# The vector c on ScalarE's queue, x's first block ahead of the first weights, gate rows through DRAM, and less VectorE work in softmax and rope, in a two-layer hybrid attention trunk

## The chip, the cores and the metric

The kernel runs on one core of one Trainium2 chip. The metric is the device time of one execution in microseconds. TensorE (PE; its weight loads are PEld), VectorE (DVE), ScalarE (ACT), GpSimd (POOL) and SyncE (SP) each run their own list of instructions in order and wait for one another by semaphores; DMAs are issued from a queue of SyncE or ScalarE.

## What is computed

Two layers over x (256 tokens of width 1024), each with its own weights. This is the reference, cut to what the change and the steps of the prediction touch:

```python
def hybrid_layer(x, c, w_ada, b_ada, w_in, ...):
    shift, scale, gate = jnp.split(c @ w_ada + b_ada, 3, axis=-1)
    u = x * (1.0 + scale[:, None, :]) + shift[:, None, :]
    h = split_cols(u @ w_in)          # 4,080 columns: three attention groups and a gate path
    ...                               # rope on most queries and keys; 4 + 6 + 6 heads
    y = (mix * jax.nn.silu(h["gate"])) @ w_out
    return layer_norm(ALPHA * x + (1.0 + gate[:, None, :]) * y, ln_g, ln_b)

def masked_softmax(s, mask):
    s = jnp.where(mask, s.astype(jnp.float32), -jnp.inf)
    m = jnp.max(s, -1, keepdims=True)
    m = jnp.where(jnp.isfinite(m), m, 0.0)
    e = jnp.where(mask, jnp.exp(s - m), 0.0)
    return e / jnp.maximum(jnp.sum(e, -1, keepdims=True), 1e-30)

def rope(x, pos):
    ...
    x1, x2 = x[..., :half], x[..., half:]
    return jnp.concatenate([x1 * cos - x2 * sin, x1 * sin + x2 * cos], -1).astype(x.dtype)
```

The three groups are DSA (4 heads, a learned index picks 64 of the keys), FoX (6 heads with a decay from a running sum) and NSA (6 heads, three branches: compressed, selected and window). All is float32.

## The kernel before

**Weights.** All weights lie in one DRAM stream `wst`, in pieces of up to 1024 columns over 128 partitions (512 KB). `stream_order` (L180) fixes their order, `load_more` (L475) issues them on SyncE's queue into 11 raw slots, a piece each time that a slot is freed. Small inputs stand in `fixed` and go on the same queue, where the order has them: x transposed in four blocks of 256 KB (`xt`, j = 0, 2, 4, 6), each behind the first projection piece of its j; tables and masks after them.

**Products.** A product in float32 is made of three passes in the rounded type: the raw piece is cast to a high half `wh` on ScalarE (`split_hi`, L519), VectorE subtracts to get the low half `wl` (`split_lo`, L534), and `mm3` (L548) multiplies high by high (L549), high by low and low by high (L550, L551). At most 8 pieces are split ahead.

**Modulation.** c comes first of all DMAs (L423), four matmuls spread it over the partitions (`spread_c`, L554), ten matmuls on zeros follow as warm-up (L575). c @ w_ada is done on VectorE: one multiplication with accumulated sum for each piece (`ada_gemv`, L583), 48 in all: the 16 of layer 0's scale and shift interleave with the first projection in order of j, the 16 of layer 1 run in `ada_second`, the 8 gate ones of each layer in `gate_task` (L613). That last one adds the bias (L618), then builds the gate row, the same 1024 values on all partitions: 16 matmuls of a broadcast column with the identity (L625) into PSUM and two copies on ScalarE (L628). The row is read by `resid` (L1251), which multiplies the output projection by it. `u_first` makes uH and the residue uL of u in layer 0 (L1370, L1372), `next_u` and `u_block` those of layer 1.

**Attention.** `attn_pair` treats two heads: scores, exponential with a running sum (`head_exp`, L680 to L697), `stats_finish` (L665: maximum with 1e-30, L667; reciprocal, L668; for NSA times its gate, L670), normalising on ScalarE (L710), transposes (L720, L724) and the product with the values (L773). There are 11 pairs in each layer; the compressed branch calls `stats_finish` too (`cmp_scores`). `rope` (L633) makes the product with the cosines (L641), two half-width products with the sines (L642, L643) and a sum (L644), 8 times in each layer.

**Order.** The instructions of all engines are written out by a planner, the class `Order`: every task is a generator that asks for an engine and a time; the planner keeps a clock for each engine from costs such as `rmm`, `cact` and `cvec`, and at each step lets the task of the best priority that can start go on (a smaller number comes first). What the tasks emit in that order is each engine's program. Priorities and the places of the loads are the entries of `PR` (L365). `split` is the priority of the two halves of a piece, as long as `nahead` pieces or more are ready ahead of TensorE (else it is -1); `gate` and `gate1` are those of `gate_task` in layers 0 and 1, `res` that of `resid`; `ada_at` says after which tile of layer 0 layer 1's modulation pieces are loaded; `tord` orders the 16 column tiles, `oq` the four quarters of the output projection.

Of the kernel before, what the change touches and what calls it, by code (L numbers as in the profile page):

```python
# [178 lines left out]

def stream_order():  # L180
# [14 lines left out]
    for l in range(DEPTH):  # L195
        if l == 0:
            ada(0, 0)
            for j in range(8):
                o.append((FIRST[j][0], 0, j))
                if j % 2 == 0:  # L200
                    o.append(("xt", j))
                o.extend((cc, 0, j) for cc in FIRST[j][1:])
                if j < 7:
                    ada(0, j + 1)
            o.append(("rope",))
        else:
            for c in PR["cord"]:
                chunk(c, l)
# [134 lines left out]
def rmm(cols, n=1):  # L343
    return n * cols / 2400.0
# [20 lines left out]
PR = dict(tout=(1, 1), tch=2, vmask=('', 'dnf'), zn='VV', upart=4, ul='VVVV', nrm='AAAA', cord='DCAB', t1q=0, cuts=(0, 512, 1024), oq=(0, 1, 2, 3), tord=(0, 1, 2, 3, 4, 5, 6, 7, 8, 9, 10, 11, 12, 13, 14, 15), gpp=(0, 1), res=-3.5, warm=10, tol=0.1, ada_at=[10, 0.5], adag_at=[[0, 0.5], [8, 1]], ow=(512, 256), aff=0.49, tw=512, nact=((0, 0), (1, 0), (0, 1), (1, 1)), pro='', gp0=(0, 1), gp1=(0, 1), acc=5, s=2, pt=1, o=3, ms=3, side=8, topk=3, idx=2, dec=0.5, cmp=1.2, nsa=1.6, dsa=1.7, fox=1.8, gate=4, gate1=6, ada=6, main=10, ev=0, split=4, nahead=2, acc1=1.5, cmp1=3, dec0=0.28, nsa1=5.08, topk1=5.9, nsa0=1.3, dec1=0.5, idx1=0.64, tord1=[2, 4, 6, 7, 0, 1, 8, 9, 5, 3, 14, 12, 10, 13, 11, 15], dsa0=1.48, oq0=(1, 0, 2, 3), cmp0=1.12, fox1=1.95, dsa1=4.17, fox0=1.48, oq1=[1, 3, 2, 0], topk0=3, tord0=[0, 1, 3, 4, 6, 7, 8, 9, 10, 11, 12, 13, 2, 5, 14, 15], idx0=2, nrm1='AAAA', nrm0='AAAA', t1q0=0, t1q1=0)  # L365
# [3 lines left out]
def trunk(ctx: ExitStack, tc: tile.TileContext, xT, x, crow, wst, bcol, lnrow, pe_b, cst, cstb, out,  # L369
# [9 lines left out]
    pp = ctx.enter_context(tc.tile_pool(name="pp", bufs=1, space=PSUM))  # L379
    ctx.enter_context(tc.manual_schedule())  # L380
# [42 lines left out]
    nc.sync.dma_start(c_row[0:P:32, 0:256], crow.rearrange("o (a b) -> (o a) b", b=256))  # L423
# [21 lines left out]
    for j in range(0, 8, 2):  # L445
        fixed["xt", j] = (xT_sb[:, j:j + 2, :], xT[:, j:j + 2, :])
# [28 lines left out]
    def load_more():  # L475
        while nload[0] < len(order):
            key = order[nload[0]]
            if key in fixed:
                nc.sync.dma_start(*fixed[key])
                dma[0] += 0.7  # L480
# [132 lines left out]
    def gate_task(l):  # L613
# [4 lines left out]
        V.tensor_tensor(m, m, bcol_sb[:, l, :, 2], op=ALU.add)  # L618
        Gr[l] = small([P, D], "row", 1, pool=act)
        for n in range(2):  # L620
            yield bank("ad")
            yield ("P", 4 * fmm(128))
            rows = ps(4, P)
            for i in range(4):
                T.matmul(rows[:, i, :], mods[l][:, 4 * n + i, 2:3].to_broadcast([P, P]), ident_f, start=True,  # L625
                         stop=True)
            yield ("A", cact(512))
            A.copy(Gr[l][:, 512 * n:512 * n + 512], rows.rearrange("p a b -> p (a b)"))  # L628
            unbank("ad")
            od.set("grow", l, n)  # L630


    def rope(dst, src, nh, dim, t, E=None):  # L633
# [8 lines left out]
        E.tensor_tensor(t3[:, :, :hf], x3[:, :, hf:], bcast(sinf[:, t, :hf], 1, nh), op=ALU.mult)  # L642
        E.tensor_tensor(t3[:, :, hf:], x3[:, :, :hf], bcast(sinf[:, t, hf:], 1, nh), op=ALU.mult)  # L643
# [59 lines left out]
    def head_pt(l, p_sb, r, a, ev, out_):  # L703
# [13 lines left out]
        yield ("P", 0.33)  # L717
# [11 lines left out]
    def attn_pair(l, kind, qT, kT, vs, obox, first, last, mask=None, cum=None, gate=None, prio=1):  # L729
# [30 lines left out]
        yield ("V", 0.35 + (0.12 if gate is not None else 0))  # L760
# [6 lines left out]
        yield ("P", fmm(128, 256))  # L767
# [19 lines left out]
    def layer(l, uH, uL):  # L787
# [111 lines left out]
        def idx_acc(acc, rl, hps, t, nk, before, ev):  # L899
# [595 lines left out]
```

## Time and profile before

| what | us |
|---|---|
| median of 3 runs | 360.07 (359.87 to 360.12) |
| the profiled execution | 359.52 |
| its span, first to last instruction | 357.7 |
| TensorE busy in it | 336.6 |
| VectorE busy | 312.4 |
| ScalarE busy | 249.8 |

The granted TensorE clock is 0.988 of full speed over the span. A matmul's recorded end is modelled and reaches into the next one, so TensorE's busy time shows where it stands still, and how dense its work is has to be read from the starts. Idle time of an engine counts only where the end hangs on it.

### The profile page before, as it was taken

The page shows a single profiled execution, that of the slowest core. Times are in us where ns is not written, and L with a number is a line of the kernel's source. Part 1 is how long each engine was busy: PE and PEld are TensorE (multiplying, and loading weights), DVE is VectorE, ACT ScalarE, POOL GpSimd, SP SyncE. Part 2 cuts the span into 40 slices and gives each one's busy share as a digit, 9 for nine tenths or more (in the row PEclk, how much of TensorE's full clock was granted, in tenths as well). Part 3 has the DMA queues.
Part 4 walks back from the last instruction along what each step waited for, and adds up shares of the span by engine and source line. Part 5 has one row for each costly group of instructions (what it writes and reads, how often), then busy time and mean ns, then how long its engine had stood idle before and what let it go on. Part 6 is the DMA issues. An engine that isn't in the chain of part 4 may idle for free.

```text
span 357.7 us, 6693 instructions
## 1 busy us (share of the span) xinstructions
PE 336.6 (94%) x2338; PEld 274.8 (77%) x2338; DVE 312.4 (87%) x811; ACT 249.8 (70%) x656; POOL 2.5 (1%) x10
## 2 busy tenths in 40 slices
PE   5899999999999999998998999999999999999990
PEld 1678789888887778695787878679798988788890
DVE  4798988999999989999999898998998989766485
ACT  3545565997868878998295875665998969998120
POOL 2000000000000000000000000000000000000000
PEclk9899999999999999999999999999999999999996
DMA  6999999996444667650588485552378724403011
GB/s 210 414 407 407 406 402 409 410 412 207 174 126 132 214 197 268 186 176 2 180 292 274 146 315 178 176 175 76 105 237 295 235 60 124 174 1 119 0 59 59
DMA packets 22073, 75.45 MB, mean 211 GB/s; under 512 B 2964, under 2 KB 3096, under 8 KB 21912
## 3 DMA queue, kind: packets, MB, share of 16 engines
q1 hardware_dynamic: 21752, 74.75, 59.5%
q8 instruction: 18, 0.29, 0.3%
q10 hardware_dynamic: 288, 0.29, 0.2%
q14 instruction: 15, 0.12, 0.1%
HBM read 73.98 MB, written 1.05 MB: 210 GB/s over the span
## 4 chain that ended last, share of the span: by engine, by line
PE 41%; DVE 7%; ACT 3%; issue 2%; DVEq 0%; ACTq 0%
PE b L549 10%; PE b L551 10%; PE b L550 10%; DVE wl L534 3%; PE b L773 2%; PE b L720 2%; PE b L739 2%; ACT p L686 1%; PE b L1030 1%; PE b L655 1%; PE b L926 1%; ACT p L710 1%; PE b L625 1%; DVE bn L1256 0%; DVE x_sb L1254 0%
## 5 line engine op out<-in xcount | busy, mean ns | idle before, releaser
L519 ACT CAST wh<-raw 128x1024 fp32r<-128x1024 f32 (+2 forms) x81 | 82.8, 1031 | 40.8 <-DMA raw<-in_wst_dram 25.0
L534 DVE TENSOR_TENSOR wl<-raw,wh 128x1024 fp32r<-128x1024 f32 (+2 forms) x81 | 96.2, 1194 | 10.2 <-ACT wh L519 4.9
L549 PE MATMUL b<-uH,wh 128*128 128x256 f32 x256 | 76.5, 299 | 0.0
L551 PE MATMUL b<-uH,wl 128*128 128x256 f32 x256 | 72.5, 283 | 0.0
L550 PE MATMUL b<-uL,wh 128*128 128x256 f32 x256 | 72.2, 282 | 0.0
L583 DVE SCALAR_TENSOR_TENSOR raw<-raw,cbc 128x1024 f32<-128x1024 f32 x48 | 58.1, 1217 | 3.2 <-DMA raw<-in_wst_dram 2.8
L549 PE MATMUL b<-wh,uH 128*128 128x512 f32 (+1 forms) x128 | 51.1, 400 | 2.3 <-ACT uH L1370 2.3
L551 PE MATMUL b<-wh,uL 128*128 128x512 f32 (+1 forms) x128 | 50.3, 393 | 2.4 <-DVE uL L1372 1.3
L549 PEld LDWEIGHTS b<-uH,wh 128*128 128x128 f32 x256 | 48.7, 190 | 3.4 <-issue 2.3
L550 PE MATMUL b<-wl,uH 128*128 128x512 f32 (+1 forms) x128 | 49.9, 389 | 0.0
L551 PEld LDWEIGHTS b<-uH,wl 128*128 128x128 f32 x256 | 48.7, 190 | 0.4 <-DVE wl L534 0.2
L550 PEld LDWEIGHTS b<-uL,wh 128*128 128x128 f32 x256 | 48.8, 191 | 0.0
L710 ACT ACTIVATE p<-p,rinv 128x128 f32<-128x128 f32 (+1 forms) x88 | 34.1, 449 | 5.6 <-DVE rinv L670 4.9
L551 PEld LDWEIGHTS b<-wh,uL 128*128 128x128 f32 x128 | 24.4, 191 | 9.0 <-DVE uL L1372 3.0
L549 PEld LDWEIGHTS b<-wh,uH 128*128 128x128 f32 x128 | 24.3, 190 | 7.5 <-ACT uH L1370 2.8
L550 PE MATMUL b<-wl,mH 128*128 128x512 f32 (+1 forms) x80 | 28.1, 351 | 1.6 <-DVE wl L534 1.6
L549 PE MATMUL b<-wh,mH 128*128 128x512 f32 (+1 forms) x80 | 28.5, 356 | 0.1
L551 PE MATMUL b<-wh,mL 128*128 128x512 f32 (+1 forms) x80 | 27.9, 349 | 0.3 <-DVE mL L1161 0.3
L550 PEld LDWEIGHTS b<-wl,uH 128*128 128x128 f32 x128 | 24.4, 191 | 4.1
L724 ACT COPY pT<-b 128x384 f32<-128x384 f32 x44 | 20.7, 478 | 4.7 <-PE b L720 4.3
L773 PE MATMUL b<-pT,vall 128*64 128x256 f32 (+1 forms) x176 | 21.7, 339 | 1.4 <-ACT pT L724 1.3
L720 PE MATMUL b<-cf,p 128*128 128x128 f32 x132 | 22.4, 281 | 0.5 <-ACT p L710 0.4
(178 smaller groups left out, 554.5 us busy)
## 6 DMA issues: line engine op xcount, KB each, us to landing
raw<-in_wst_dram SPq DMA_DIRECT2D x120, 512.0 KB, 4.9
raw<-in_wst_dram SPq DMA_DIRECT2D x7, 480.0 KB, 9.8
lnr<-in_lnrow_dram SPq DMA_DIRECT2D x4, 512.0 KB, 6.2
raw<-in_wst_dram SPq DMA_DIRECT2D x4, 448.0 KB, 4.4
xT_sb<-in_xT_dram SPq DMA_DIRECT2D x4, 256.0 KB, 9.5
x_sb<-in_x_dram SPq DMA_DIRECT2D x1, 1024.0 KB, 11.4
out_dram<-x_sb SPq DMA_DIRECT2D x3, 256.0 KB, 2.2
cf<-in_cst_dram SPq DMA_DIRECT2D x1, 384.0 KB
```

Source lines behind the costliest of these rows:

```text
L519: A.copy(h[:, :n], loaded[key])
L534: (G if on_pool else V).tensor_tensor(lo[:, :n], raw, h[:, :n].bitcast(F32), op=ALU.subtract)
L549: T.matmul(o, ah, bh, start=start, stop=False)
L550: T.matmul(o, ah, bl, start=False, stop=False)
L551: T.matmul(o, al, bh, start=False, stop=stop)
L583: V.scalar_tensor_tensor(w, w, 1.0, cbc, op0=ALU.mult, op1=ALU.mult, accum_out=mods[l][:, j, h:h + 1])
L625: T.matmul(rows[:, i, :], mods[l][:, 4 * n + i, 2:3].to_broadcast([P, P]), ident_f, start=True, stop=True)
L710: A.mul(blk, blk, r[:, t, a:a + 1])
L720: T.transpose(pt[:, i, :], p_sb[:, P * i:P * i + P], ident)
L724: A.copy(pT, pt.rearrange("p a b -> p (a b)"))
L739: T.matmul(sp[a][:, P * t:P * t + nk], qT[r, t * P:(t + 1) * P], kT[r, :nk], start=True, stop=onv and cum is None, skip_group_check=True)
L773: T.matmul(O[64 * a:64 * a + 64, P * kt:], vs(a, kt), outs[a][0][:, 256 * kt:256 + 128 * kt], start=(first and kt == 0), stop=(last and kt ...
```

## The change

- c's DMA is issued on ScalarE's queue, ahead of bcol's, and no longer on SyncE's.
- x transposed comes in five blocks, of 1, 2, 2, 2 and 1 of its eight parts (j = 0; 1 and 2; 3 and 4; 5 and 6; 7); the first, 128 KB, is issued ahead of the first projection weights, the others behind those of their first j.
- The gate row: after the bias is added, the 1024 values (8 in each partition, 3 apart) are written to a DRAM tile on SyncE's queue; about 4.5 us later by the planner's clock the tile is read back on the same queue, broadcast to all partitions (512 KB). The matmuls of L625 and the copies of L628 are gone.
- stats_finish takes the maximum with 1e-30 only for the compressed branch, where a row can be empty.
- rope makes one product of full width with the sines, over the two halves in reverse order, in place of two.
- The planner: TensorE's cost of a matmul gets 12 ns more, some costs of VectorE and TensorE change, the indexer takes its buffers one by one (its matmuls stay), and these entries of PR change:

| entry | before | after |
|---|---|---|
| res | -3.5 | -0.5 |
| gate, gate1 | 4, 6 | 0.52, 2.89 |
| split, nahead | 4, 2 | 5, 1 |
| ada_at | 10, then every 0.5 | 8, then every 0.5 |
| nsa0, nsa1 | 1.3, 5.08 | 1.72, 0.13 |
| dsa0 | 1.48 | 0.12 |
| idx0, idx1 | 2, 0.64 | 1.87, 8.55 |
| cmp0, dec1 | 1.12, 0.5 | 1.39, 0.43 |
| oq0 | 1, 0, 2, 3 | 1, 3, 0, 2 |
| tord0 | 0, 1, 3, 4, 6 to 13, 2, 5, 14, 15 | 0, 1, 3, 2, 4 to 12, 14, 15, 13 |
| tord1 | 2, 4, 6, 7, 0, 1, 8, 9, 5, 3, 14, 12, 10, 13, 11, 15 | 0, 2, 4, 6, 7, 1, 8, 9, 5, 3, 14, 10, 12, 13, 11, 15 |

```diff
+XT = {0: 1, 1: 3, 3: 5, 5: 7, 7: 8}
...
             for j in range(8):
+                if j == 0:
+                    o.append(("xt", 0))
                 o.append((FIRST[j][0], 0, j))
-                if j % 2 == 0:
+                if j and j in XT:
                     o.append(("xt", j))
...
-    return n * cols / 2400.0
+    return n * (cols / 2400.0 + 0.012)
...
-    nc.sync.dma_start(c_row[0:P:32, 0:256], crow.rearrange("o (a b) -> (o a) b", b=256))
+    A.dma_start(c_row[0:P:32, 0:256], crow.rearrange("o (a b) -> (o a) b", b=256))
...
+        row = hbm.tile([D], F32, tag="gate", name=nm("gate"), bufs=DEPTH)
+        nc.sync.dma_start(row.rearrange("(j p) -> p j", p=P), m)
+        od.ev["gw", l] = od.now + 4.5
+        yield until(("gw", l))
+        yield ("G", 0.01)
         Gr[l] = small([P, D], "row", 1, pool=act)
+        nc.sync.dma_start(Gr[l], row.unsqueeze(0).to_broadcast([P, D]))
         for n in range(2):
-            yield bank("ad")
-            yield ("P", 4 * fmm(128))
-            rows = ps(4, P)
-            for i in range(4):
-                T.matmul(rows[:, i, :], mods[l][:, 4 * n + i, 2:3].to_broadcast([P, P]), ident_f, start=True,
-                         stop=True)
-            yield ("A", cact(512))
-            A.copy(Gr[l][:, 512 * n:512 * n + 512], rows.rearrange("p a b -> p (a b)"))
-            unbank("ad")
-            od.set("grow", l, n)
+            od.ev["grow", l, n] = od.now + 4.0
...
-        E.tensor_tensor(t3[:, :, :hf], x3[:, :, hf:], bcast(sinf[:, t, :hf], 1, nh), op=ALU.mult)
-        E.tensor_tensor(t3[:, :, hf:], x3[:, :, :hf], bcast(sinf[:, t, hf:], 1, nh), op=ALU.mult)
+        x4, t4 = (v.rearrange("p h (u d) -> p h u d", d=hf) for v in (x3, t3))
+        s4 = bcast(sinf[:, t, :].rearrange("p (u d) -> p u d", d=hf), 1, nh)
+        E.tensor_tensor(t4, x4[:, :, ::-1, :], s4, op=ALU.mult)
...
-    def stats_finish(st, gate=None):
+    def stats_finish(st, gate=None, empty=False):
         r = small([P, *st.shape[1:]], f"rinv{len(st.shape)}", 6)
-        V.tensor_scalar(r, st, 1e-30, None, op0=ALU.max)
-        V.reciprocal(r, r)
+        if empty:
+            V.tensor_scalar(st, st, 1e-30, None, op0=ALU.max)
+        V.reciprocal(r, st)
...
-            r = stats_finish(mx, gates[:, t, 0, :])
+            r = stats_finish(mx, gates[:, t, 0, :], True)
```

## Rows read from the trace of the kernel before

**Rows 1.** The page's first two parts: busy time of each engine with its share of the span and its instructions, and the busy share of the DMA engines in tenths in 40 equal slices of the span.
```profile
PE 336.6 (94%) x2338; PEld 274.8 (77%) x2338; DVE 312.4 (87%) x811; ACT 249.8 (70%) x656; POOL 2.5 (1%) x10
...
DMA  6999999996444667650588485552378724403011
```

**Rows 2.** Busy time by stretch of the span. Columns: the stretch, its length, then for PE, PEld, DVE, ACT and POOL the busy us with the instructions in brackets, the granted clock, the DMA share and GB/s.
```profile
70.00:90.00 20.00, 20.00 (x164) 17.26 (x164) 19.17 (x50) 16.70 (x46) 0.00 (x0) 1.00 0.87 321
...
130.00:150.00 20.00, 19.20 (x158) 13.89 (x154) 19.57 (x51) 16.73 (x55) 0.00 (x0) 1.00 0.72 236
150.00:170.00 20.00, 18.88 (x121) 15.31 (x119) 19.84 (x38) 18.25 (x39) 0.00 (x0) 1.00 0.29 102
170.00:190.00 20.00, 18.10 (x105) 15.47 (x105) 19.69 (x41) 11.93 (x20) 0.00 (x0) 1.00 0.72 244
190.00:210.00 20.00, 19.06 (x96) 16.14 (x97) 18.63 (x34) 14.11 (x33) 0.00 (x0) 1.00 0.70 240
...
300.00:340.00 40.00, 39.92 (x282) 33.40 (x281) 25.38 (x71) 29.83 (x86) 0.00 (x0) 1.00 0.23 80
```

**Rows 3.** The timeline of the first 12 us. Columns: start, length, engine (SPq is SyncE's queue), line, operation, names, shapes, count, and in brackets the engine's idle time before it with what ended it.
```profile
0.73 0.68 SPq L423 DMA_DIRECT2D c_row<-in_crow_dram  x1
...
1.47 1.33 SPq L488 DMA_DIRECT2D raw<-in_wst_dram  x3
...
3.46 1.24 PE L562 MATMUL b<-c_row,ones 1*128 1x256 f32 x8 [3.46 <-DMA c_row<-in_crow_dram]
...
7.92 1.04 ACT L519 CAST wh<-raw 128x1024 fp32r<-128x1024 f32 x1 [2.59 <-DMA raw<-in_wst_dram]
8.00 0.16 DVE L595 TENSOR_TENSOR mod<-mod,bcol_sb 128x2 f32<-128x2 f32 x1
8.99 1.23 DVE L534 TENSOR_TENSOR wl<-raw,wh 128x1024 fp32r<-128x1024 f32 x1 [0.83 <-ACT wh L519]
10.04 0.60 ACT L1370 ACTIVATE uH<-xT_sb,mod 128x256 fp32r<-128x256 f32 x1 [1.08 <-DMA xT_sb<-in_xT_dram]
...
10.69 0.64 PE L549 MATMUL b<-wh,uH 128*128 128x512 f32 x1 [2.34 <-ACT uH L1370]
...
11.13 0.63 PE L550 MATMUL b<-wl,uH 128*128 128x512 f32 x1
```

**Rows 4.** The timeline of the end: the last matmul and the last DMA issue.
```profile
349.28 0.28 PE L551 MATMUL b<-wh,mL 128*128 128x256 f32 x1
...
354.43 0.35 ACTq L1327 DMA_DIRECT2D out_dram<-x_sb  x1
```

**Rows 5.** The chain of work that ended last, between 300 and 335 us: start, length, what.
```profile
308.06 0.89 PE b L625 x8
...
329.09 1.09 PE b L625 x8
```

**Rows 6.** Busy time by stretch of line L625 alone: PE, PEld, granted clock, DMA share, GB/s.
```profile
130.00:150.00 20.00, 2.11 (x16) 1.94 (x16) 1.00 0.72 236
```

**Rows 7.** The DMA view of the first 12 us: GB/s in 40 slices of 0.3 us, and the packets, MB and share of 16 engines of ScalarE's DMA queue, whose only transfer there is bcol.
```profile
GB/s 0 0 0 0 0 13 64 15 126 68 96 341 328 410 396 423 396 396 423 423 423 423 389 294 143 130 123 89 123 248 355 399 435 422 416 449 410 423 437 423
...
q10 hardware_dynamic: 144, 0.02, 1.4%
```

**Rows 8.** Groups of instructions by line, VectorE: busy us, mean ns of one, then idle time before them.
```profile
L641 DVE TENSOR_TENSOR roped<-chunk,cf 128x288 f32<-128x288 f32 (+3 forms) x16 | 7.6, 476 | 0.1
...
L643 DVE TENSOR_TENSOR ropet<-chunk,cf 128x144 f32<-128x144 f32 (+3 forms) x16 | 5.0, 313 | 0.0
L642 DVE TENSOR_TENSOR ropet<-chunk,cf 128x144 f32<-128x144 f32 (+3 forms) x16 | 5.0, 312 | 0.0
...
L667 DVE TENSOR_SCALAR rinv<-st 128x4 f32<-128x4 f32 x22 | 3.6, 163 | 3.5 <-ACT p L686 3.5
```

**Rows 9.** The timeline of TensorE from 155 to 192 us, those lines of it before which TensorE stood idle.
```profile
162.74 0.50 PE L551 MATMUL b<-wh,mL 128*128 128x512 f32 x1 [0.29 <-DVE mL L1161]
...
164.21 0.50 PE L550 MATMUL b<-wl,mH 128*128 128x512 f32 x1 [0.75 <-DVE wl L534]
...
172.38 0.50 PE L550 MATMUL b<-wl,mH 128*128 128x512 f32 x1 [0.84 <-DVE wl L534]
...
181.20 0.63 PE L1390 MATMUL b<-cf,x_sb 128*128 128x128 f32 x4 [0.51 <-issue]
...
190.56 0.47 PE L551 MATMUL b<-wh,uL 128*128 128x448 f32 x1 [1.10 <-DVE uL L1416]
```

**Rows 10.** Busy time by stretch of TensorE alone at the start: busy us, granted clock, DMA share, GB/s.
```profile
10.00:12.00 2.00, 1.31 (x3) 0.72 1.03 422
12.00:14.00 2.00, 2.00 (x6) 0.50 1.02 415
14.00:16.00 2.00, 2.00 (x10) 0.92 1.03 418
```

**Rows 11.** Busy time by stretch of line L583, the modulation's products on VectorE, each with a short read of its sum: busy us, granted clock, DMA share, GB/s.
```profile
50.00:70.00 20.00, 3.64 (x6) 1.00 1.03 408
70.00:90.00 20.00, 2.45 (x4) 1.00 0.87 321
...
130.00:150.00 20.00, 10.88 (x18) 1.00 0.72 236
```

**Rows 12.** DMA issues from 56 to 90 us: names, queue, count, KB each, median us from issue to landing.
```profile
raw<-in_wst_dram SPq DMA_DIRECT2D x16, 512.0 KB, 10.2
```

More of the change, by code (lines that the diff above doesn't have):

```diff
@@ L379, in trunk @@
     pp = ctx.enter_context(tc.tile_pool(name="pp", bufs=1, space=PSUM))
+    hbm = ctx.enter_context(tc.tile_pool(name="hbm", bufs=1, space=bass.MemoryType.DRAM))
     ctx.enter_context(tc.manual_schedule())
@@ L444, in trunk @@
         fixed["w2", l] = (w2_sb[:, l, :], wst[:, o:o + n])
-    for j in range(0, 8, 2):
-        fixed["xt", j] = (xT_sb[:, j:j + 2, :], xT[:, j:j + 2, :])
+    for j in XT:
+        fixed["xt", j] = (xT_sb[:, j:XT[j], :], xT[:, j:XT[j], :])
     def cv(name):
@@ L716, in head_pt @@
         yield lock("pT")
-        yield ("P", 0.33)
+        yield ("P", 0.38)
         pt = ps(3, P)
@@ L759, in attn_pair @@
         yield until(*evs)
-        yield ("V", 0.35 + (0.12 if gate is not None else 0))
+        yield ("V", 0.18 + (0.16 if gate is not None else 0))
         r = stats_finish(st, gate)
@@ L766, in attn_pair @@
         yield until(*evs)
-        yield ("P", fmm(128, 256))
+        yield ("P", 0.85)
         if first:
@@ L897, in layer, with idx_acc @@
         mask = small([P, 384], "dmask", 1, dt=BF16)
-        def idx_acc(acc, rl, hps, t, nk, before, ev):
+        def idx_acc(acc, rl, hp, t, nk, before, ev):
             if before:
                 yield until(before)
-            for i, hp in enumerate(hps):
-                yield ("V", cvec(nk, 2) + 0.11)
-                for a in range(2):
-                    h = hp + 4 * a
-                    V.scalar_tensor_tensor(acc, rl[:, i, a, :], iw_sb[:, t, h:h + 1],
-                                           fill[:, 2 * P - nk:] if h == 0 else acc, op0=ALU.mult, op1=ALU.add)
+            yield ("V", cvec(nk, 2) + 0.2)
+            for a in range(2):
+                h = hp + 4 * a
+                V.scalar_tensor_tensor(acc, rl[:, a, :], iw_sb[:, t, h:h + 1],
+                                       fill[:, 2 * P - nk:] if h == 0 else acc, op0=ALU.mult, op1=ALU.add)
             od.release("t2k")
@@ L934, in indexer @@
                     evs.append((nm("ia"),))
-                    hps = [h0 + per * i + j for j in range(per)]
-                    od.spawn(idx_acc(acc, rl, hps, t, nk, before, evs[-1]), pr("idx", l))
+                    od.spawn(idx_acc(acc, rl, h0 + i, t, nk, before, evs[-1]), pr("idx", l))
             yield until(*evs)
@@ L1023, in compress @@
             for m0 in range(0, 16, 4):
-                yield ("P", 0.62)
+                yield ("P", 0.8)
                 if m0 == 0:
@@ L1264, in resid @@
             mu = mv[:, 0:1]
-            yield ("V", 0.2)
+            yield ("V", 0.4)
             V.bn_aggr(mv, stats[:, t].rearrange("p n s -> p (n s)"))
@@ L1363, in u_first @@
         for j in range(8):
-            yield until(("mod", 0, j), ("raw", ("xt", j - j % 2)))
+            yield until(("mod", 0, j), ("raw", ("xt", max(k for k in XT if k <= j))))
             yield lock("sg")
```

28 lines of the change are left out of this document (14 added, 14 removed).

## The prediction

> **What bounds the kernel now.** I read the page's first two parts, then busy time by stretch, then the two ends of the timeline. On the page TensorE is busy 336.6 us of the span of 357.7, VectorE 312.4, ScalarE 249.8 [rows 1]. By stretch two kinds are to be told apart [rows 2]: those in which TensorE is full and VectorE has room (300 to 340: 39.92 of 40 us against 25.38), and 150 to 210, where TensorE lacks 1.12, 1.90 and 0.94 us, 3.96 together, while VectorE stands at 19.84 and 19.69 of 20. So the end is set by TensorE's own work, and around the change of layers by VectorE. Outside lie the start, 10.69 us to the first matmul of the stream [rows 3], and the tail: the last matmul begins at 349.28 and the last output is issued at 354.43 [rows 4].
>
> **The gate rows.** The change removes 32 matmuls of L625 and four ScalarE copies. Sixteen of the matmuls stand in the chain that ended last, in stretches where nothing but TensorE is late: 0.89 and 1.09 us [rows 5], 1.98 us. The sixteen of layer 0 take 2.11 us of recorded time in 130 to 150 [rows 6], where VectorE has 19.57 of 20 us and TensorE itself lacks 0.80 [rows 2], so they pay in full only if VectorE gets less to do as well, which it does (next part). Recorded ends overlap a little; I take 3.5 us together, with 2.0 (layer 1 alone) and 4.1 as ends. In exchange come, in each layer, one write of 1024 single values to DRAM and one 512 KB read. For the write the nearest row is the 192-byte packets of bcol on queue 10: 144 packets in 1.4% of 16 engines over 12 us, 19 ns each [rows 7]; 64 on each of 16 engines are 1.2 us. From above, the slowest packets of the trace are those of the first block of xT, 2 KB each (two blocks of 256 values in a partition) at 89 GB/s over 16 engines, 0.37 us: 64 of them are 24 us. The size of the packets speaks for the lower end, and I take it. On the path I put write and read at 0, because the row is first used by L1251, after the output projection has begun, and the loads have slack: after 90 us the DMA mostly stands at 4 to 7 tenths [rows 1]. What it costs if that cover is gone is the second rival.
> The Trainium skill, page "DMA: Bandwidth & Descriptors", section "Rules for kernel authors", speaks against this write: a last dimension that isn't contiguous becomes one descriptor for each element; and under "Specifications" it has transfers below 512 B done as read-modify-write. No run so far shows such a write, and the page has no price for one; by the row the sum is as below, by the rule the write would be the dear one, and the sum that of the second rival, nothing gained.
>
> **VectorE's small operations.** stats_finish loses the maximum of L667 in the 22 attention pairs, 22 x 0.163 = 3.6 us. In rope two half-width products of 0.313 and 0.312 us become one of full width; the nearest row for that is the full-width product L641, 0.476 us, so 16 ropes save 16 x 0.149 = 2.4 us [rows 8]. If the reversed operand ran at half that rate they would cost 16 x 0.33 = 5.3 us instead; I take the row, since L641 also reads a broadcast table. Together 6.0 us, half of it in each layer. It counts only where VectorE is the late one: the waits of TensorE in 155 to 192 are 0.29, 0.75, 0.84, 0.51 and 1.10 us, four of them on VectorE results (the one named "issue" I leave open), 3.5 us together [rows 9]. The 3 us that VectorE is spared in layer 0 lie before them. I take 1.5 us; ends 0 and 3.5.
>
> **The start.** Now c is issued on SyncE's queue at 0.73 us for 0.68, and the first weights only at 1.47. TensorE waits for c until 3.46, mod is ready at 8.00 + 0.16, ScalarE casts the first weights at 7.92, and uH waits 1.08 us more, for xT, until 10.04 [rows 3]. After the change the weights' issue moves up by at most 0.74 us, and c goes in front of bcol and of the table load on ScalarE's queue, which both have until the copy of c. The first block of x shrinks to 128 KB and passes the first AB weights. Its price is not in the trace at this size: while the old one of 256 KB moved, between 6.9 and 8.7 us, the rate fell from 423 to as little as 89 GB/s [rows 7]. At 410 GB/s the new block takes 0.3 us, and if the fall goes by rows, which stay 128, up to 2.1. So the AB weights, cast at 7.92 now, land between 7.92 - 0.74 + 0.3 = 7.5 and 9.3. With 1.04 us for the cast and 1.23 for wl the second matmul (L550, wl with uH) can begin between 9.8 and 11.6, against 11.13 now [rows 3]; uH, with xT here before mod, is no longer late, and wl takes its place. The middle is 10.7, a gain of 0.4. The loads behind it come about 0.7 us earlier too, which shortens the waits for the next blocks; I add 0.3. Gain 0.7; ends a loss of 0.5 and a gain of 1.6.
> The clock is apart from that: after the warm-up matmuls TensorE stands still 2.34 us [rows 3], and the granted clock is 0.72 in 10 to 12 us, 0.50 in 12 to 14 and 0.92 in 14 to 16 [rows 10]. That is 1.12 + 2.0 + 0.32 = 3.4 us at the 1.2 GHz level, half of it lost, 1.7 us. I leave it as it is, for the start stays about where it was.
>
> **The new order.** The tile costs, the priorities and the order of tiles change the whole written order, and no row of before tells what it gives. Earlier gate products (priority 4 to 0.52) move VectorE work that now lies in 130 to 150 (10.88 us of L583) towards 50 to 90 (3.64 us and 2.45) [rows 11], and the products of layer 1's modulation move up behind them, away from the full stretch. Against it stands that 70 to 90 has VectorE at 19.17 of 20 already [rows 2]. I take 0; ends a gain of 2 (half of 3.96) and the loss of the third rival.
>
> **Sum.** 3.5 + 1.5 + 0.7 + 0 = 5.7 us. The profiled execution took 359.52, its span 357.7; 359.52 - 5.7 = 353.8. The median of the three runs, 360.07, is 0.55 above that execution, so the forecast is 354.4.
>
> **The rivals.** First, everything relieved: TensorE's five waits go altogether (3.5), the first matmuls come early enough that the clock doesn't fall (1.7), the gate rows give 4.1 and the start 0.7: 10.0 us, 350.1. For it: all three engines lose work. Against it: VectorE remains above 9 tenths in every stretch of layer 0.
> Second, the change doesn't bring what it says, through SyncE's queue. The read of the gate row must wait until the write has landed, and every weight load written behind it waits with it. In 56 to 90 us a load takes 10.2 us from issue to landing [rows 12], where the planner grants the write 4.5; the queue then stands 10.2 - 4.5 = 5.7 us, and if TensorE runs out of pieces that is all of the gain: 360.1; with the write at its upper price it would stand 24 us and the time be longer. Against it: the small packets, and the pieces split ahead, up to 8.
> Third, slower. The eight gate products of layer 0, 1.2 us each (2.45 us for two in 70 to 90 [rows 11]), are now taken before the low halves wl, whose priority outside need falls from 4 to 5 and which become urgent only when fewer than 1 piece, not 2, is ahead. Each time TensorE comes to a piece whose wl stands behind such a product it waits up to 1.2 us. Now 0.75 and 0.84 are the two such waits [rows 9]. From five new ones on (6.0 us) the gain is gone; seven make 8.4 - 5.7 = 2.7 us, 362.8.
>
> **How the numbers follow.** Forecast 354.4 with 0.61, of which 0.02 reaches within 0.2% of before; everything relieved 0.17; the queue 0.08; the order 0.14, of which 0.02 within 0.2%. About 0.2%, 0.7 us, is what the measurement can tell from no change. So faster 0.59 + 0.17 + 0.02 of the second rival = 0.78, same 0.02 + 0.06 + 0.02 = 0.10, slower 0.12. The range runs from 349.8, which leaves out half of the first rival, to 360.8, which takes in the second at its lower price and leaves out most of the third: 0.19 outside.
>
> **What would show it.** Right: no L625 and L628; TensorE's busy time down by some 4 us; uH no longer waiting for xT, and L550 waiting for wl at the start; the waits in the change of layers below 2.5 us; the tail as it is, some 8 us from the last matmul to the end of the span. Wrong: an issue of the gate row's read after which no load follows for 5 us, with ScalarE's casts waiting for raw behind it; new waits of L550 for wl in 50 to 130; a rope product of 0.9 us; a first matmul later than 11 us.

## The result and the profile after

The changed kernel takes 363.68 us (363.16 to 364.51), the kernel before on the same chip 359.99: ratio 1.011, 95% interval 1.0097 to 1.0122. The forecast was a gain of 5.7 us, the result is a loss of 3.7, outside the range. The profiled execution took 364.51, its span is 362.7.

The page of after, part 1, which answers to the first of [rows 1].
```profile
PE 338.9 (93%) x2306; PEld 276.2 (76%) x2306; DVE 308.6 (85%) x773; ACT 246.3 (68%) x652; POOL 2.5 (1%) x10
```
VectorE and ScalarE have lost 3.8 and 3.5 us of work (of VectorE's the prediction expected 6.0), and TensorE has lost 32 matmuls, yet its busy time is 2.3 us higher: part of its work ran at the half clock. The instructions were taken out as planned, the time was lost elsewhere. I take three places one by one.

**The start.** The timeline of after, the rows that answer to [rows 3].
```profile
0.74 1.09 ACTq L429 DMA_DIRECT2D c_row<-in_crow_dram  x1
...
1.87 0.35 ACTq L437 DMA_DIRECT2D bcol_sb<-in_bcol_dram  x1
...
4.57 1.24 PE L568 MATMUL b<-c_row,ones 1*128 1x256 f32 x8 [4.57 <-DMA c_row<-in_crow_dram]
...
7.09 0.26 DVE L595 TENSOR_SCALAR bcol_sb<-bcol_sb 128x16 f32<-128x16 f32 x2 [5.82 <-DMA bcol_sb<-in_bcol_dram]
...
10.53 0.16 DVE L601 TENSOR_TENSOR mod<-mod,bcol_sb 128x2 f32<-128x2 f32 x1
...
10.72 0.60 ACT L1374 ACTIVATE uH<-xT_sb,mod 128x256 fp32r<-128x256 f32 x1 [4.27 <-DVE mod L601]
11.23 1.03 ACT L525 CAST wh<-raw 128x1024 fp32r<-128x1024 f32 x1
...
12.31 0.50 PE L555 MATMUL b<-wh,uH 128*128 128x512 f32 x1 [2.25 <-ACT wh L525]
13.57 0.80 PE L556 MATMUL b<-wl,uH 128*128 128x512 f32 x1 [0.76 <-DVE wl L540]
15.05 0.80 PE L557 MATMUL b<-wh,uL 128*128 128x512 f32 x1 [0.69 <-DVE uL L1376]
```
c and bcol, issued beside the stream of weights, land late: VectorE has c's copies and the whole modulation behind bcol, and the last step of mod begins at 10.53, not 8.00. On ScalarE uH now stands ahead of the first cast, so wh waits for mod as well. TensorE comes to its third matmul 3.4 us later than before (11.64 there). Thin work follows, and the granted clock falls; the windows (columns as in [rows 2]) answer to [rows 10].
```profile
12.00:14.00 2.00, 0.94 (x2) 0.47 (x2) 1.71 (x2) 1.90 (x4) 0.00 (x0) 0.80 1.03 404
14.00:16.00 2.00, 1.31 (x3) 0.83 (x3) 2.00 (x4) 0.78 (x1) 0.00 (x0) 0.50 1.03 408
16.00:18.00 2.00, 2.00 (x6) 1.54 (x5) 2.00 (x5) 0.68 (x2) 0.00 (x0) 0.50 1.02 409
18.00:20.00 2.00, 2.00 (x6) 1.52 (x6) 1.58 (x3) 1.80 (x3) 0.00 (x0) 0.50 1.03 408
```
At the 1.2 GHz level are (1 - 0.80) x 4 + 3 x 2 = 6.8 us, against 3.4 before. The last of the 192 matmul passes of the first projection begins at 59.31, against 56.83: 2.5 us late.

**The gate row's write.** SyncE's queue in after, layer 1.
```profile
278.11 0.38 SPq L626 DMA_DIRECT2D gate<-mod  x1
280.19 3.32 SPq L494 DMA_DIRECT2D raw<-in_wst_dram  x3
288.24 0.33 SPq L631 DMA_DIRECT2D row<-gate  x1
```
The write of 4 KB is issued at 278.11, and the read that waits for it at 288.24: 10.1 us (in layer 0 88.63 and 98.77, 10.1 again). What it does to the engines is seen a few us later, in the timelines of ScalarE, VectorE and TensorE:
```profile
292.48 1.05 ACT L525 CAST wh<-raw 128x1024 fp32r<-128x1024 f32 x1 [4.04 <-DMA raw<-in_wst_dram]
293.43 0.44 ACT L1086 ACTIVATE pcv<-pcv 128x90 f32<-128x90 f32 x2
...
293.74 0.25 DVE L1088 TENSOR_TENSOR pcv<-pcv,cf 128x90 f32<-128x90 f32 x1 [2.71 <-ACT pcv L1086]
...
295.24 0.42 PE L1097 MATMUL b<-cf,pc 128*96 128x128 f32 x2 [1.57 <-DVE pc L1091]
```
Read it downwards: the cast waits 4.04 us for the first weight piece issued behind the write, at 280.19; the exponential L1086 stands behind that cast on ScalarE though its operands are there; VectorE waits 2.71 us for it and TensorE 1.57 us for VectorE. A late piece that nobody on TensorE needed yet stopped TensorE, through the order of ScalarE's list.

The DMA view of 279 to 281 us: packets, then the queue with its packets, MB and share of 16 engines, then the issue of that piece with its size and the time to its landing.
```profile
DMA packets 1040, 0.00 MB, mean 2 GB/s; under 512 B 1040, under 2 KB 1040, under 8 KB 1040
...
q1 hardware_dynamic: 1040, 0.00, 23.9%
...
raw<-in_wst_dram SPq DMA_DIRECT2D x1, 512.0 KB, 12.3
```
All 1024 values (and 16 packets more) are recorded in these 2 us, with 23.9% of 16 engines, some 7 ns each. Yet the read that waits for them isn't issued before 288.24, and the piece behind them takes 12.3 us to land. The packets' rows don't show what the write costs; the landings do.

**The change of layers.** TensorE's waits over the span, some of them (us in total, times, longest).
```profile
PE b L1394 <- issue: 1.9, 1, 1.9
PE b L1097 <- DVE pc L1091: 1.6, 1, 1.6
...
PE b L556 <- DVE wl L540: 0.8, 1, 0.8
```
L1394 transposes the new x, which `resid` makes; on VectorE two wl of 1.0 us (178.97 and 180.36; in before one) stand between its last steps, TensorE stands still 1.9 us, and the clock falls behind it (0.50 in 184 to 186, shown below beside the run of rows in after). The only wait for a wl is the one at the start.

### The profile page after: what moved, and what is told of

Its sections match the earlier page's. It is cut to its first block, busy times and chain, and to the rows that moved or that the text cites. A ratio compares the mean times of both kernels' runs of the same rounds, so it can differ in the third digit from the quotient of the medians.

```text
span 362.7 us, 6588 instructions
## 1 busy us (share of the span) xinstructions
PE 338.9 (93%) x2306; PEld 276.2 (76%) x2306; DVE 308.6 (85%) x773; ACT 246.3 (68%) x652; POOL 2.5 (1%) x10
## 4 chain that ended last, share of the span: by engine, by line
PE 48%; DVE 24%; ACT 18%; DMA 3%; issue 3%; another core or an unknown queue 0%; DVEq 0%; ACTq 0%
PE b L555 14%; PE b L557 14%; PE b L556 13%; DVE wl L540 6%; DVE raw L589 4%; ACT p L716 3%; DMA raw<-in_wst_dram 3%; ACT wh L525 3%; ACT p L692 3%; DVE nmx L699 2%; DVE iacc L950 2%; ACT p L703 2%; ACT pT L730 2%; PE b L779 1%; DVE iacc L911 1%
## 5 line engine op out<-in xcount | busy, mean ns | idle before, releaser
L726 PE MATMUL b<-cf,p 128*128 128x128 f32 x132 | 23.6, 283 | 1.6 <-ACT p L716 1.4
L779 PE MATMUL b<-pT,vall 128*64 128x128 f32 (+1 forms) x176 | 24.4, 340 | 0.6 <-ACT pT L730 0.4
```

The costliest lines, as they stand in the source:

```text
L726: T.transpose(pt[:, i, :], p_sb[:, P * i:P * i + P], ident)
L779: T.matmul(O[64 * a:64 * a + 64, P * kt:], vs(a, kt), outs[a][0][:, 256 * kt:256 + 128 * kt], start=(first and kt == 0), stop=(last and kt ...
```

## The experiments

Times are medians in us; in brackets the ratio to the kernel before on the same chip with its 95% interval (that kernel: 359.75 to 359.96).

### Each part alone, the planner free to redraw

The first three undo or do one part. **c back on SyncE in after:** 363.28 (1.0095, 1.0066 to 1.0125).
```diff
-    A.dma_start(c_row[0:P:32, 0:256], crow...)
+    nc.sync.dma_start(c_row[0:P:32, 0:256], crow...)
```


> The changed kernel with one line undone: c's DMA first on SyncE's queue again. The written order of the engines is the same. Theory A (the start costs some 2.5 us because c and bcol land late beside the weights, and the new order some 5 more, against some 3.7 that the gate rows give): 361.2 us, first matmul of the stream before 10.7 us. Theory B (the gate row's way through DRAM holds the queue and is the whole loss; the start cost is made good later): 363.7, no change from the changed kernel.

The first matmul begins at 10.73 again and the first projection ends 1.0 us earlier than in after, but by the first matmul on mH only 0.1 us of that is left (162.84 against 162.96): 0.7 are left at 66 us and 0.1 from 106 on, where TensorE has waited for pT longer than in after (1.0 us against 0.4 over the span). The four executions lie in two pairs, 362.3 and 364.3, so the 0.4 of the median is no measured gain.

**c on ScalarE in before, nothing else:** 359.15 (0.9983, 0.9974 to 0.9992).

> The kernel before with one line changed: c's DMA on ScalarE's queue, ahead of bcol. The written order is the same. Theory A: 362.2 us, bcol lands after 6 us where it landed at 2.6. Theory B: 360.0.

mod is late here too (10.74) and the first matmul 0.9 us later, but the weights start 0.7 us earlier, and the first projection ends 0.5 us earlier than in before. Neither theory had a gain. The end of that stage hangs on the stream of weights, not on its first matmul: its last pass begins at 56.16 to 56.44 in all four runs that have the start of before with c on ScalarE, x's block ahead or not, and at 56.79 or later in those with c on SyncE.

**stats_finish and rope of the change in before:** 358.12 (0.9951, 0.9934 to 0.9967).

> The kernel before with the smaller stats_finish and the one product of full width in rope; the planner's costs stay, so the written order is the same but for the instructions left out. Both theories: faster, by 0.5 to 1.5 us (358.5 to 359.5); VectorE's busy time down by 6.0 us, and the rope product at 0.48 us. If the reversed operand is slow, 0.9 us and no gain.

A gain of 1.75, a little above what was expected. The groups of VectorE by line show the price of the product with the reversed operand, 477 ns, as that of L641 with the straight one (also 477):
```profile
L644 DVE TENSOR_TENSOR ropet<-chunk,cf 128x288 f32<-128x288 f32 (+3 forms) x16 | 7.6, 477 | 0.0
```
But VectorE's busy time falls by 3.6 us (312.4 to 308.8), not by 6.0, and TensorE's waits between 155 and 192, which were to shrink, are those of [rows 9]: 0.29, 0.74, 0.85, 0.50 and 1.14, three of them here:
```profile
163.21 0.50 PE L550 MATMUL b<-wl,mH 128*128 128x512 f32 x1 [0.74 <-DVE wl L534]
171.38 0.49 PE L550 MATMUL b<-wl,mH 128*128 128x512 f32 x1 [0.85 <-DVE wl L534]
...
189.56 0.47 PE L551 MATMUL b<-wh,uL 128*128 128x448 f32 x1 [1.14 <-DVE uL L1419]
```
By the starts of the same matmuls, TensorE comes out 0.1 us ahead of before at 94 us, 0.3 at 97, 0.7 at 109, 1.0 at 150 and 190 and 1.4 from 261 on. Each step from 97 on stands at a wait of TensorE for p or pT; before 150 us ScalarE's p waits for `stats_finish`'s rinv (3.9 us from 90 on in before, 2.4 here).

**Only the planner's entries, costs and indexer, with the parts of before:** 370.39 (1.0291, 1.0276 to 1.0307). **Only the gate rows through DRAM, in before:** 373.75 (1.0388, 1.0368 to 1.0407). **All parts, planner's entries of before:** 374.16 (1.0405, 1.0389 to 1.042).

> The kernel before with only the planner's part of the change: its new costs, priorities, tile orders and places of loads; c, x's blocks, gate rows, softmax and rope as before. Theory A: 365.4 us (363.7 - 2.5 for the start + 3.7 for the gate rows + 0.5). Theory B: 360.0.

> The kernel before with only the gate rows sent through DRAM (priorities and costs as before). Theory C (the new order is the loss, the parts are gains): 356.3 us, the 3.7 us of TensorE's work; SyncE's queue stands 10 us twice and nobody runs out of pieces. Theory B (the way through DRAM costs what it saves): 360 or more, with ScalarE's casts waiting for raw pieces behind the write.

> All parts of the change (c, x's blocks, gate rows, softmax, rope) with the planner's costs, priorities and places of before. Theory C: 357 us: 360 - 3.7 - 1.75 and the start's loss of 2.5. If the parts need the new order: 363 or more.

Each half of the change loses far more alone than both together, so the account is not additive as long as the planner redraws. Neither theory had such losses for the first of the three, where no row goes through DRAM; the loss is the order's: one wait of 3.4 us for a wl, 1.9 for p, 1.4 for x_sb. In the second TensorE waits 6.5 us at once for pT, behind ScalarE's cast.

**Before with c on ScalarE, gate rows through DRAM and fewer VectorE operations, x as it was:** 372.02 (1.0327, 1.0304 to 1.0349). **After with `res` back at -3.5:** 362.33 (1.0062, 1.0038 to 1.0085). **After with c and the blocks of x as in before:** 375.78 (1.0433, 1.0392 to 1.0474).

> The same without the new blocks of x: the kernel before with c on ScalarE's queue, gate rows through DRAM, the smaller softmax and rope. Theory C: 353.9 us, 360 - 0.7 - 1.75 - 3.7, and the faster of all; x's block ahead of the weights is then 2.5 to 3 us of loss with c on ScalarE's queue. If x's blocks cost nothing: the same as the run with them.

> The changed kernel with one priority undone: resid at -3.5 again. Theory C, with the priority of resid as what makes TensorE wait 2.0 us at the change of layers and lets its clock fall after it (another 1.7 us): 361 us, no fall of the clock near 184. If the wait stems from another entry: 363.7.

> The changed kernel with the start undone: c on SyncE's queue and x's blocks of before. If the start's 2.5 us at the end of the first projection reach the end: 361.2. If they are made good at the change of layers: 363.7.

The first of these and the run with all parts and the entries of before differ in x's blocks alone: with the five blocks the planner draws the two places of after, uH ahead of the first cast and a product of the modulation ahead of uL, and the first projection's last pass begins at 59.70 instead of 56.33. With the new entries and the old blocks it is 56.95. So it is the blocks, through the planner, that make the start late, not the entries.
`res` gives 1.35 back, with an uncertainty of some 0.9 to either side, between what was expected with it and without. It moves one product of `resid` on VectorE; TensorE still waits 1.6 us before L1394, and 0.7 more for x_sb, but in the profiled execution the clock doesn't fall there. The third is the warning of this series: putting the start back, which costs the changed kernel 2.5 us, made it 12 us slower, where 361.2 or 363.7 was expected; with four loads in place of five the planner redraws every list. Of this series only c and VectorE's operations are priced, for they change nothing that the planner sees.

### The price of the write

**The gate column transposed on TensorE and written as 8 rows of 512 B**, in before (365.1: 1.0142, 1.0125 to 1.0159) and in after (360.43: 1.0014, 1.0005 to 1.0024), and **the read on GpSimd's queue**, in before with the single values (373.44: 1.0375, 1.0354 to 1.0396).
```diff
-        nc.sync.dma_start(row.rearrange("(j p) -> p j", p=P), m)
+        T.transpose(gp[0:8, :], m, ident)
+        A.copy(gt, gp[0:8, :])
+        nc.sync.dma_start(row.rearrange("(j p) -> j p", p=P), gt)
```


> The kernel before with the gate row through DRAM, but the 1024 values are transposed on TensorE first (one matmul and one ScalarE copy in each layer) and written as 8 rows of 512 B; order entries of before. Theory E (it is the single values of the write that hold SyncE's DMA rings for some 10 us): some 357 us, 3.7 - 0.3 us less than before, the read issued under 4 us after the write. Theory F (any trip through DRAM on this queue holds the loads, by the wait of the read or by the read's 512 KB): over 365.

> The changed kernel with the write as 8 rows of 512 B after a transpose. Theory E with the new order, which sends the first write at 89 us, when 8 pieces are split ahead: the 10 us are covered there, so 362 to 364. If the write costs as much here as in the old order: 352 to 355.

> The kernel before with the gate row through DRAM as in the change, only the read back is issued on GpSimd's queue, so that SyncE doesn't wait for the write and can go on issuing loads. If SyncE's wait is the loss: 357 us. If the rings themselves stand behind the 1024 values: 370 or more, with the loads issued behind the write landing 10 us late as before.

The same 4 KB in 8 pieces: 8.65 us less in before, 3.25 less in after. The first has the time of theory F and the early read of theory E, 1.2 us behind the write; the runs with the order held, below, decide for E. The second lies between what was expected either way. In after the engines' lists stay the same but for the transposes, the copies and one exchange behind the second write, and two loads go ahead of that write; by the starts of the same matmuls the profiled executions part by 1.3 us in 99 to 116, by 1.1 at the change of layers and by 1.9 in 288 to 318. The read on another queue: nothing. From that run's DMA view (the write, with its time to landing) and its timelines, SyncE's queue, GpSimd, ScalarE, and under them ScalarE of the run with the read on SyncE:
```profile
gate<-mod SPq DMA_DIRECT2D x1, 4.0 KB, 12.5
...
131.36 0.39 SPq L621 DMA_DIRECT2D gate<-mod  x1
131.84 16.89 SPq L489 DMA_DIRECT2D raw<-in_wst_dram  x11
...
144.41 0.66 POOL L626 DMA_DIRECT2D row<-gate  x1 [141.31 <-PE b L718]
...
153.42 1.04 ACT L520 CAST wh<-raw 128x1024 fp32r<-128x1024 f32 x1 [6.94 <-DMA raw<-in_wst_dram]
```
```profile
153.50 1.04 ACT L520 CAST wh<-raw 128x1024 fp32r<-128x1024 f32 x1 [6.95 <-DMA raw<-in_wst_dram]
```
SyncE now goes on issuing loads from 131.84 on, and ScalarE gets its piece at 153.42 as at 153.50 with the read in SyncE's list. Freeing the list gains nothing: the write lands 12.5 us after its issue, the loads that are already issued stand behind the 1024 values on the DMA queue (the second, issued at 132.46, lands after 14.6 us), and from 132 to 144 us the DMA moves 6 to 61 GB/s, then 336 and more. Whether the write on a queue of its own would leave them free was not tried.

The run of rows in after, a window at the change of layers, and under it that of after:
```profile
184.00:186.00 2.00, 2.00 (x20) 2.00 (x18) 1.97 (x6) 1.59 (x5) 0.00 (x0) 1.00 0.45 68
```
```profile
184.00:186.00 2.00, 2.00 (x11) 2.00 (x10) 2.00 (x3) 1.25 (x3) 0.00 (x0) 0.50 0.25 102
```
The wait of 1.9 us is in both, the fall of the clock in after alone.

### The order held

Now the parts are emitted at other places of the code but the planner is asked for the same times, banks and loads as in before. Every engine's list then is that of before, but for the instructions of the part. For the gate rows:
```diff
             yield bank("ad")
             yield ("P", 4 * fmm(128))
-            rows = ps(4, P)
-            for i in range(4): T.matmul(rows[:, i, :], ...)
+            if n == 0: T.transpose(gp[0:8, :], m, ident)
             yield ("A", cact(512))
-            A.copy(Gr[l][:, 512 * n:512 * n + 512], ...)
+            if n == 0: A.copy(gt, gp[0:8, :]); nc.sync.dma_start(<row>, gt)
+            else:      nc.sync.dma_start(Gr[l], <row on all partitions>)
```
**Rows of 512 B:** 358.92 (0.9972, 0.9961 to 0.9982). **1024 single values:** 372.29 (1.0343, 1.0322 to 1.0363).

> Before with the gate rows through DRAM, the column transposed on TensorE and written as 8 rows of 512 B, but the planner is asked for the same times and banks as before, so that every engine's list stays as it is but for the 32 matmuls and 4 copies that go, 2 transposes, 2 small copies and 4 DMAs. Theory A (what costs is the order that the planner redraws when its clock changes; the part itself is a gain): the prediction's 3.5 us, 356.4, between 355.8 and 357.9. Theory B (the way through DRAM itself makes TensorE wait, whatever the order): 359 or more, as the 365.1 of the same rows with a redrawn order.

> Before with the gate rows through DRAM as 1024 single values, as in the change, but in the order of before. It prices the write itself: the rings stood behind it for 10 to 12 us. Theory A (the loss is the order's): 356 to 357.5. Theory B (the loss is the rings': pieces come late, ScalarE's casts wait for them and TensorE for the casts): 362 to 374, with a wait of several us on TensorE some 15 us behind the write, as in the run that gave 373.75.

These two differ by the write (with its transpose and small copy) alone, and by 13.4 us. SyncE's queue and the first use of the row, in the run of rows:
```profile
139.11 0.30 SPq L632 DMA_DIRECT2D gate<-gt  x1
139.51 0.35 SPq L489 DMA_DIRECT2D raw<-in_wst_dram  x1
140.36 0.33 SPq L634 DMA_DIRECT2D row<-gate  x1
...
333.09 0.69 DVE L1257 TENSOR_TENSOR t2k<-b,row 128x512 f32<-128x512 f32 x1 [2.08 <-DMA row<-gate]
```
and in the run of single values, with ScalarE, TensorE, a window in which nearly every engine stands still and one in which the clock has fallen:
```profile
131.64 0.39 SPq L627 DMA_DIRECT2D gate<-mod  x1
132.12 0.53 SPq L489 DMA_DIRECT2D raw<-in_wst_dram  x1
143.87 0.33 SPq L629 DMA_DIRECT2D row<-gate  x1
...
151.05 1.04 ACT L520 CAST wh<-raw 128x1024 fp32r<-128x1024 f32 x1 [4.24 <-DMA raw<-in_wst_dram]
...
152.80 1.54 PE L774 MATMUL b<-pT,vall 128*64 128x256 f32 x6 [4.79 <-ACT pT L725]
...
148.00:150.00 2.00, 0.01 (x1) 0.00 (x0) 0.00 (x0) 0.00 (x0) 0.00 (x0) 1.00 0.99 348
...
152.00:154.00 2.00, 1.20 (x6) 0.76 (x6) 1.88 (x3) 2.00 (x10) 0.00 (x0) 0.52 1.04 426
...
331.30 0.43 SPq L627 DMA_DIRECT2D gate<-mod  x1
344.76 0.33 SPq L629 DMA_DIRECT2D row<-gate  x1
...
349.56 0.69 DVE L1252 TENSOR_TENSOR t2k<-b,row 128x512 f32<-128x512 f32 x1 [11.59 <-DMA row<-gate]
```
From the write's issue to the read's it is 1.25 us by rows and 12.2 (layer 0) and 13.5 us (layer 1) by values. The piece issued right behind the write lands 4.4 us later by rows (issued at 139.51) and 13.2 by values (132.12). In layer 0 the pieces behind it come late and starve ScalarE's cast, with pT behind it and TensorE behind pT, and the clock falls once more; TensorE is 7 us behind from there to its end. In layer 1 the row itself is late: VectorE waits 11.59 us for it in the tail, where nothing covers that, and the span is 370.1 - 356.9 = 13.2 us longer in all. The changed kernel's `gate1` of 2.89 puts this second write at 278 us, where the row is not yet wanted: its order spares it this loss, and of the 13.4 us the write costs it 3.25.

Theory A fell for the single values. For the rows the time lies between the two theories, just below B's 359: a gain, but of 0.9 us where 3.5 were expected.

**Rows, c on ScalarE and fewer VectorE operations:** 356.88 (0.9919, 0.9903 to 0.9934). **x's first 128 KB first, alone:** 360.04 (1.0004, 0.9994 to 1.0013). **All of these together:** 356.87 (0.9923, 0.991 to 0.9936).
```diff
+            if key == (FIRST[0][0], 0, 0):
+                nc.sync.dma_start(xT_sb[:, 0:1, :], xT[:, 0:1, :])
...
-        fixed["xt", j] = (xT_sb[:, j:j + 2, :], xT[:, j:j + 2, :])
+        a = max(j, 1)
+        fixed["xt", j] = (xT_sb[:, a:j + 2, :], xT[:, a:j + 2, :])
```


> The rows of the run before this, plus c on ScalarE's queue and the fewer VectorE operations, all in the order of before. Theory A: 356.4 less 0.7 and 1.75, the two parts' own measured gains: 354.0, a version faster than both kernels. Theory B: above 357.

> Before with the first 128 KB of x loaded ahead of the first projection piece and the second 128 KB where the block of 256 KB was, all engines in the order of before. If the 2.5 us that the changed kernel is late at the end of the first projection come from x's block going ahead: 361.5 to 362.4, the first matmul about a us later. If they come from c and bcol behind one another on ScalarE's queue and from the new order: 359.2 to 360.2, and the first matmul no later than 10.7.

> All parts of the change (with the gate row as rows of 512 B) in the order of before: the run of rows, fewer VectorE operations and c on ScalarE (356.88), plus x's first 128 KB ahead of the first projection piece. If the parts are additive in a given order: 356.9 plus 0.2, between 356.5 and 357.5. If x's block and c together make the start late: 359 or more.

With the order held the parts nearly add up: 0.7 + 1.75 + 0.9 = 3.35 expected from them, 2.94 measured. x's first block ahead, with the rest of x in its old places, changes nothing. The last is the version that beats both kernels, by 2.9 us the one before and by 6.8 the changed one.

### The start of the changed kernel

**After with rows of 512 B, and of its order two neighbouring pairs exchanged:** the first cast ahead of uH, and uL ahead of the next modulation product; 358.86 (0.9983, 0.9973 to 0.9992).
```diff
 # ScalarE              # VectorE
-uH<-xT_sb,mod          -raw,mod<-raw,cbc
 wh<-raw                 uL<-sg,uH
+uH<-xT_sb,mod          +raw,mod<-raw,cbc
```


> The changed kernel with the gate row as 8 rows of 512 B (360.43), and of its whole order two neighbouring pairs at the start exchanged, as the kernel before has them: the first cast wh ahead of uH on ScalarE, and uL ahead of the next product of the modulation on VectorE; all else in its order. Theory A (the start's 2.5 us come from these two places, which the planner redrew when x's block got ahead): uL's matmul begins at some 12.6 us in place of 15.05, and the time falls by 2 to 2.5 us, to 358.0 to 358.5. Theory B (x's block ahead of the weights, or c and bcol on one queue, make the start late through the loads): within 0.5 us of 360.4.

```profile
8.63 1.04 ACT L526 CAST wh<-raw 128x1024 fp32r<-128x1024 f32 x1 [2.26 <-DMA raw<-in_wst_dram]
10.88 0.60 ACT L529 ACTIVATE uH<-xT_sb,mod 128x256 fp32r<-128x256 f32 x1 [1.21 <-DVE mod L607]
...
11.53 0.50 PE L559 MATMUL b<-wh,uH 128*128 128x512 f32 x1 [1.42 <-ACT uH L529]
...
12.48 0.50 PE L561 MATMUL b<-wh,uL 128*128 128x512 f32 x1
...
179.89 0.63 PE L1415 MATMUL b<-cf,x_sb 128*128 128x128 f32 x4 [1.88 <-issue]
```
uL's matmul begins at 12.48, the clock stays at 1.00 over the start, and the first projection ends at 56.79, 2.5 us earlier than without the exchange and as early as in before. So the lateness against before sits in these two places of the lists, not in the loads; 0.4 to 0.6 us are left to the 56.16 to 56.44 of the runs with the start of before and c on ScalarE. At the end 1.6 of the 2.5 are left: in the profiled execution (360.14) TensorE reaches the transposes of x earlier, waits the same 1.88 us for `resid`, and here the clock does fall behind it (0.50 in 182 to 184). Nine of the twelve executions lie between 358.6 and 359.1, three between 360.0 and 360.2. Only one has a profile, and the mean granted clock of the rest (0.985 to 0.991 in the three, 0.987 to 0.996 in the nine) doesn't part them, so whether that fall does is open.

## Why the prediction was wrong

The account, run by run: before 359.8; the parts in the order of before, with a quick write, -2.9; the redrawn order +3.6 (360.43 - 356.87; x's last blocks and the indexer's buffers change with it), of which the two exchanges at the start are 1.6; 1024 single values in place of 8 rows +3.25 (363.68 - 360.43). Together +3.9, measured +3.7. Each term starts where the one before ends, so that the sum comes out is no test of it; what shows the terms are the runs that hold the order.

**The step that failed first** is in the gate rows: "The size of the packets speaks for the lower end, and I take it. On the path I put write and read at 0". The write takes 10.1 us in the changed kernel and 12 to 13.5 in the order of before, inside the bounds of 1.2 and 24 and far from the end that I took. The row that I scaled by size, bcol's packets, was a read of 192-byte pieces from DRAM; nothing in the trace wrote single values. And the kind of row was wrong: a packet's recorded time is no price of such a write, for the 1024 packets are recorded with some 7 ns each, less than the 19 that I took, while the write lands 12.5 us after its issue (in the run with the read on GpSimd's queue). Why, no run here shows. The Trainium skill, page "DMA: Bandwidth & Descriptors", section "Rules for kernel authors", had it: a last dimension that isn't contiguous becomes one descriptor for each element. The trace agrees in number: between the two runs with the order held the packets under 512 B go from 3012 to 5076, two times 1024 and a few. The page gives no time for it; here it is some 10 us for 1024.
And "On the path I put write and read at 0" looked only at who reads the row. The loads behind the write were the path. The second rival had the victims right (pieces late, casts waiting for raw) and gave the cause to SyncE's list; the run with the read on GpSimd's queue showed that the queue behind the values holds the pieces as long when the list is free.

**The gate rows' gain** was sized 3.5 and is 0.9 with the order held. By the starts of the same matmuls in both traces TensorE is 0.2 us late before the 16 matmuls of layer 0, 0.95 early at 139 us and 0.6 late from 148 on: layer 0 loses 0.4. It waits for pT and p on ScalarE, 0.8 + 0.7 us in 138 to 152, where before had 0.4 + 0.4. The reservation in that step, that layer 0 pays in full only if VectorE gets less to do, missed the cause: against the run with the fewer VectorE operations alone, the run with both is 1.15 us further ahead at 139 and has lost all of it by 147. There TensorE waits 1.2 us for pT, behind a cast that waits 0.68 us for a weight piece, issued at 139.22 behind the row's read. The pieces are late because SyncE has only one list, and the write in it waits for the transposed column (in us in total, times, longest; the run of rows):
```profile
SPq L632 <- ACT gt L631: 17.7, 2, 13.9
```
From 124.77 to 139.11 no load is issued there; before issues six in that time. So with the quick write SyncE's list, the second rival's cause, does hold back the loads, at the write and not at the read. Layer 1 gave 1.3 of its 1.98 (0.6 late at 307 us, 0.7 early from 330).

**VectorE's operations:** 1.5 predicted, 1.75 measured, and the reversed operand at the row's price. The number is right, the way to it is not. VectorE is spared 3.6 us, not 6.0: recorded lengths overlap, and in before it is 0.55 us from the start of L642 to that of the sum (57.49 to 58.04), against 0.48 with the one product (57.55 to 58.03). And the five waits that the term was taken from stayed; the gain came from waits for p and pT, three before 150 us and one at 255. That the sizes meet is luck.

**The start:** a gain of 0.7 predicted, 2.5 lost at the end of the first projection. c's move alone is worth 0.7, but all of it by the earlier weights, which I had at 0.3; the first matmuls, which I had 0.4 earlier, come 0.9 later. What failed is "which both have until the copy of c": bcol, issued at 1.87, stops VectorE until 7.09, and c's copies and mod stand behind it. And "uH ... is no longer late, and wl takes its place" took the lists as they were; the planner, given the five blocks, put uH ahead of the cast. With the two exchanged that loss is gone. The clock, which I left as it was, fell for 6.8 us in place of 3.4; with the two exchanged it doesn't fall there at all.

**The new order** is the other step that failed: put at 0 with "no row of before tells what it gives". It costs 3.6 with the same parts. The third rival gave 362.8, near the measured time, by another mechanism: gate products ahead of wl. The only wait for a wl in after is 0.8 us at the start; what the order lost are the two places at the start, and `resid` behind other work (1.9 us before L1394, where before has 0.5; how much of it is `res` is open). The rest of the 3.6 is not traced; between the profiled executions of the run with the exchanges and of the one that holds the order (360.14 and 356.54), 0.4 us part them at the end of the first projection, 2.7 at layer 1's first matmul and 3.6 at the end. That near hit is chance.

## What to carry to other kernels

Where the instruction lists are drawn by a planner from costs, price a part with the order held: ask the planner for the old times and exchange only what is emitted. Here the gate row with the quick write costs 5.1 us with the planner free (365.1) and gains 0.9 with the order held (358.92), and only with the order held could the write be priced, at 13.4 us there.
Before a small column goes to DRAM, transpose it so that it goes in rows; and ask of each slow DMA not who reads its result but which transfers are issued behind it, and which in-order list waits for those.

## What the runs showed of the hardware that was not expected

- A write of 1024 single values of 4 B takes 10.1 to 13.5 us until the transfer that waits for it is issued; the same 4 KB as 8 rows of 512 B, 1.25 us. The profile records the 1024 packets with some 7 ns each, so they don't show it. The first weight piece behind it in layer 1 of the changed kernel is issued at 280.19 and takes 12.3 us to land; behind the rows such a piece takes 4.4 (issued at 139.51).
- Two transfers of 4 and 24 KB on ScalarE's queue beside the stream of weights: c, issued at 0.74, is used at 4.57 (3.46 from SyncE's queue ahead of the weights), and bcol, issued at 1.87, at 7.09.
- The first matmul 0.9 us later and the end of the stage 0.5 us earlier, from the same change (c on ScalarE in before): with the DMA share at 1.03 in 10 to 60 us, the stream's 0.7 us counted here, TensorE's start didn't.
